# Feed-forwards 2 to 4 of a Conformer trunk: seven of nine inner blocks by seven products, with the weight sums of four of them made in advance

## The chip, the cores and the metric

The kernel runs on one core of a Trainium2 chip. The time is the device time of one execution in microseconds; the time before is the median of three runs, and one further execution was profiled. Everything below is float32: each matrix product is made as three TensorE matmuls of numbers split into a high and a low part.

## The reference

The input is 256 tokens of 1024 features. Two layers follow one another; each is feed-forward, mixer, feed-forward, with residual additions, and a final norm ends it. So there are four feed-forwards, numbered 1 to 4 here. The mixer of the first layer is a convolution module (between feed-forwards 1 and 2), that of the second is latent attention (between 3 and 4).

```
def swiglu_ffn(h, w1, w3, w2):                 # w1, w3: 1024 x 2816, w2: 2816 x 1024
    return (jax.nn.silu(h @ w1) * (h @ w3)) @ w2

for i in range(DEPTH):                          # DEPTH = 2
    h = h + 0.5 * swiglu_ffn(rmsnorm(h, ffn_norm1[i]), ffn1_w1[i], ffn1_w3[i], ffn1_w2[i])
    m = rmsnorm(h, mix_norm[i])
    h = h + (conv_module(m, ...) if i % 2 == 0 else mla(m, ...))
    h = h + 0.5 * swiglu_ffn(rmsnorm(h, ffn_norm2[i]), ffn2_w1[i], ffn2_w3[i], ffn2_w2[i])
return rmsnorm(h, final_norm)
```

## The kernel before, in words

**Weights.** All weights come in blocks of 128 x 2048 floats (1 MB). A list `blocks` names them in the order in which they are used: per feed-forward 22 blocks of w1 and w3 (the gates), then 11 blocks of w2, each of which holds two groups of 128 rows. `load` brings a block from HBM into a `raw` tile through the SP queue; ScalarE casts it to `hi` (L171) and VectorE subtracts to get `lo` (L175). There are four `raw` buffers and four `hi`/`lo` pairs, used in rotation. `weights` hands a block to the products and, by `load_ahead`, issues in program order the loads of the following blocks for which `hi`/`lo` slots are left.

**Splitting a product.** `mm3` makes one product of 128 x 128 by 128 x 512 by three matmuls: high by low, high by high, low by high (L284, L287, L288).

**Gates.** In six steps `c` (five of 512 columns, a last one of 256) the kernel makes u for w1 and w3 and both halves of the tokens (tb = 0, 1), then the gated value g. `turn` transposes g: VectorE turns 32 x 32 squares (L645), four transfers write the result to a DRAM tile `gd` (L649), one reads it back as `gb` (L651). Then it is split into `Gh` and `Gl` (L624, L625), the left operands of the second product. Step `c` yields the operands of the w2 blocks 2c and 2c+1.

**Second product.** `Rows` accumulates in four PSUM banks (two token halves by two column halves). A plain block (`block`) takes eight products, 24 matmuls. The blocks in `FAST`, which are 0, 2, 4, 6 and 8, are made by seven products (`fast`), 21 matmuls, after the scheme of Strassen and Winograd: the 2 x 2 split of tokens and rows by rows and columns. It needs sums of weight quarters and differences of gate quarters, and four extra banks p1, p5, q7, q6. `load_fast` makes the sums of weights in a second `raw` tile, `sums`: one operation on POOL for two of them (L185) and two adds on VectorE (L186, L187), and then splits both tiles (L193, L194), so that such a block takes two `raw` buffers and two `hi`/`lo` slots. `combine` makes the differences of gates on POOL (L632). After the last fast block `fold` adds the extra banks into h, with ScalarE (L572), VectorE (L574 to L579) and POOL (L573 to L580). The last two blocks, 9 and 10, are made bank by bank in `finish`, each followed by an add into h (L587) and by pieces of the next stage's norm.

**Order.** A planner orders the instructions of every engine by a simulated time line; `order` adds an ordering between two instructions of one engine by hand without a wait, and `behind` keeps the work on weights behind the last few urgent pieces. Each engine and the SP queue then run their instructions strictly in that order. All transfers spoken of here are issued by SP.

**End.** In feed-forward 4 the next stage is `Final`: it fetches the final gain `gf` once into its own tile (L484), and each piece of the result is made in one of four tiles `hg`.

Of the kernel before, what the change touches and what calls it, by code (L numbers as in the profile page):

```python
# [45 lines left out]
FAST = (0, 2, 4, 6, 8)  # L46
# [41 lines left out]
def trunk(ctx: ExitStack, tc: tile.TileContext, x, xt, pos, invf, gains, gfin, wdw,  # L88
# [27 lines left out]
    conv_block = {}  # L116
    for i in range(2):
# [35 lines left out]
    def load(src, pieces=1):  # L153
        if isinstance(src, tuple) and src[0] == "fast":
            return load_fast(src[1])
        if isinstance(src, tuple):
# [21 lines left out]
    def load_fast(src):  # L178
# [7 lines left out]
        behind(nc.vector.tensor_add(t[:, 2, :], t[:, 0, :], v[:, 3, :]))  # L186
        behind(nc.vector.tensor_add(t[:, 3, :], t[:, 2, :], v[:, 2, :]))  # L187
# [23 lines left out]
    def slots(b):  # L211
        return 2 if isinstance(blocks[b], tuple) and blocks[b][0] == "fast" else 1
# [267 lines left out]
    class Final:  # L480
        def __init__(self, act):
            self.act = act
            self.gf = act.tile([P, D], F32, tag="gf", name="gf")
            nc.sync.dma_start(self.gf, gfin.partition_broadcast(P))  # L484

            self.e = [None] * NT
            self.n = [0] * NT
            self.y = {}

        def piece(self, tb, c):  # L490

            n = c.stop - c.start
            t = self.act.tile([P, 512], F32, tag="hg", name=uid("hg"), bufs=4)
# [26 lines left out]
    class Rows:  # L520
        def __init__(self, zh, zl, nk, last=False, sh=None, sl=None):
            self.zh, self.zl, self.nk, self.last = zh, zl, nk, last
            self.sh, self.sl = sh, sl
# [24 lines left out]
        def fast(self, i):  # L548

            n = FAST.index(i)  # L550
# [6 lines left out]
            for o, key, (ah, al), (hi, lo), q in (  # L557
                    (self.p[0], "p1", z(f, 0), raw, 0), (self.o[0, 0], (0, 0), z(f + 1, 0), raw, 2),
                    (self.o[0, 1], (0, 1), s(2), raw, 3), (self.p[2], "p5", z(f, 1), sums, 0),
                    (self.p[3], "q7", s(1), sums, 1), (self.p[1], "q6", s(0), sums, 2),  # L560
                    (self.o[1, 0], (1, 0), z(f + 1, 1), sums, 3)):
                c = slice(q * 512, q * 512 + 512)
                mm3(o, ah, al, hi[:, c], lo[:, c], self.begin(key), isinstance(key, str) and i == FAST[-1])
            if i == FAST[-1]:
                self.fold()
# [46 lines left out]
    def ffn(X, make_next, beside=lambda: None):  # L612
        with tc.tile_pool(name=uid("ffn"), bufs=1) as act:
            return ffn_in(act, X, make_next, beside)

    def ffn_in(act, X, make_next, beside):
        Gh = act.tile([P, NF, S], F32R, tag="Gh", name=uid("Gh"))
        Gl = act.tile([P, NF, S], F32R, tag="Gl", name=uid("Gl"))
        Sh = act.tile([P, 3 * len(FAST), P], F32R, tag="Sh", name=uid("Sh"))
        Sl = act.tile([P, 3 * len(FAST), P], F32R, tag="Sl", name=uid("Sl"))  # L620
# [6 lines left out]
        def combine(i, b0, b1):  # L627

            n = FAST.index(i)
            sx = act.tile([P, 4, P], F32, tag="sx", name=uid("sx"))  # L630
            v = sx.rearrange("p s (i q) -> p s i q", q=32)
            sub = lambda o, a, b: nc.gpsimd.tensor_tensor(o, a, b, op=ALU.subtract)  # L632
# [4 lines left out]
            split(Sh[:, 3 * n:3 * n + 3, :], Sl[:, 3 * n:3 * n + 3, :], sx[:, :3, :])  # L637
            split(Gh[:, 2 * i, tbs(1)], Gl[:, 2 * i, tbs(1)], sx[:, 3, :])

        def turn(c, tb, w, g):  # L640
# [10 lines left out]
            nc.sync.dma_start(b[:, :w], d)  # L651
# [3 lines left out]
            t0 = 0  # L655
            if tb == 1 and 2 * c in FAST:
                t0 = 1
                combine(2 * c, first[c], bv)
            f = slice(4 * c + t0, 4 * c + n)
            gh, gl = (G_[:, f, tbs(tb)].rearrange("p t (i q) -> p t i q", q=32) for G_ in (Gh, Gl))  # L660
            split(gh, gl, bv[:, t0:])
# [49 lines left out]
        o = Rows(Gh, Gl, NF, make_next is Final, Sh, Sl)  # L711
        for i in range(NF // 2 - 2):
            (o.fast if i in FAST else o.block)(i)
# [663 lines left out]
```

## Time and profile before

| what | value |
|---|---|
| median of three runs | 924.54 us (923.88 to 925.65) |
| the profiled execution | 923.62 us |
| its span (first to last instruction) | 921.8 us |
| TensorE clock granted | 0.999 of full |
| HBM read, written | 178.17 MB, 12.58 MB |
| feed-forward 2: gates until, second product until | about 404, about 460 us |
| feed-forward 3: gates until, second product until | about 581, about 640 us |
| feed-forward 4: gates until, second product until | about 858, about 915 us |

The page gives for each engine the time in which it was busy; PE is TensorE, PEld its weight loads, DVE is VectorE, ACT ScalarE, POOL GpSimd, SPq the SP queue. In the timelines a row gives the start, the duration, the engine, the line of the kernel, the operation, the tiles written and read, the size, the count, and in brackets how long the engine had been idle and what ended that. Matmuls overlap: one takes 0.39 us from start to end, but the next starts after about 0.23. The second columns of a windows row are busy times in us within the stretch.

### The profile page before, as it was taken

The numbers are of one execution on the slowest core, as the hardware profiler recorded it, in microseconds if no ns is written. First come the engines' busy times: TensorE is split into PE (matmuls) and PEld (weight loads), VectorE is DVE, ScalarE is ACT, GpSimd is POOL, SyncE is SP. The second block draws the span as 40 slices with busy tenths as digits, with TensorE's granted clock in tenths as the row PEclk, the third lists the DMA queues.
The fourth block names the chain that finished last, engine by engine and source line by source line (L and its number), as shares of the span: only waits on it lengthen the run. The fifth ranks groups of instructions, "written<-read, shape, count | busy, mean of one in ns | idle before, by whom it ended". The sixth has DMA issues, their size and how long they took to land.

```text
span 921.8 us, 12383 instructions
## 1 busy us (share of the span) xinstructions
PE 909.6 (99%) x4293; PEld 755.5 (82%) x4293; DVE 680.9 (74%) x1052; ACT 539.7 (59%) x940; POOL 226.4 (25%) x337
## 2 busy tenths in 40 slices
PE   9999999999999999999999999999999999999997
PEld 6888888898958888888888888888998788888886
DVE  5776877689977666777976667978667476667876
ACT  6964556568877455455474544655666475444643
POOL 1101232379941100232300003224200000013223
PEclk9999999999999999999999999999999999999999
DMA  9976656653307676556756775656441557774651
GB/s 342 350 276 226 203 180 222 240 183 138 138 22 283 244 255 240 189 161 228 299 205 238 252 244 153 228 209 214 183 183 60 186 202 251 246 239 150 219 183 47
DMA packets 60399, 191.58 MB, mean 208 GB/s; under 512 B 11184, under 2 KB 33328, under 8 KB 40752
## 3 DMA queue, kind: packets, MB, share of 16 engines
q1 hardware_dynamic: 59760, 190.09, 58.9%
q8 instruction: 34, 0.56, 0.2%
q10 hardware_dynamic: 576, 0.69, 0.2%
q14 instruction: 29, 0.24, 0.1%
HBM read 178.17 MB, written 12.58 MB: 207 GB/s over the span
## 4 chain that ended last, share of the span: by engine, by line
PE 72%; DVE 8%; DMA 8%; ACT 4%; issue 3%; POOL 3%; SPq 1%; POOLq 0%; ACTq 0%; DVEq 0%
PE u L288 15%; PE u L287 15%; PE u L284 15%; DVE lo L175 5%; PE o L284 3%; PE o L287 3%; PE o L288 3%; PE gate L738 3%; DMA raw<-in_f2w 3%; DMA raw<-in_f1w 3%; PE u L738 3%; POOL sums L185 3%; PE o L978 2%; ACT hi L171 1%; DVE lo L194 1%
## 5 line engine op out<-in xcount | busy, mean ns | idle before, releaser
L175 DVE TENSOR_TENSOR lo<-raw,hi 128x1024 fp32r<-128x1024 f32 (+1 forms) x246 | 296.3, 1240 | 74.4 <-ACT hi L171 74.1
L171 ACT CAST hi<-raw 128x1024 fp32r<-128x1024 f32 (+1 forms) x250 | 247.9, 1046 | 147.7 <-PE u L288 107.9
L288 PE MATMUL u<-hi,Xl 128*128 128x512 f32 x688 | 267.8, 390 | 0.7 <-DVE Xl L345 0.7
L284 PE MATMUL u<-lo,Xh 128*128 128x512 f32 x688 | 268.1, 390 | 0.1
L287 PE MATMUL u<-hi,Xh 128*128 128x512 f32 x688 | 267.7, 389 | 0.0
L288 PEld LDWEIGHTS u<-hi,Xl 128*128 128x128 f32 x688 | 129.1, 188 | 28.2 <-DVE Xl L345 1.6
L284 PEld LDWEIGHTS u<-lo,Xh 128*128 128x128 f32 x688 | 129.2, 188 | 27.3 <-DVE lo L175 0.5
L287 PEld LDWEIGHTS u<-hi,Xh 128*128 128x128 f32 x688 | 129.2, 188 | 26.6
L185 POOL TENSOR_TENSOR sums<-raw 128x1024 f32<-128x1024 f32 x20 | 54.2, 2710 | 162.4 <-DMA raw<-in_f2w 52.7
L284 PE MATMUL o<-lo,Gh 128*128 128x512 f32 (+1 forms) x236 | 91.5, 388 | 0.7 <-DVE lo L175 0.7
L287 PE MATMUL o<-hi,Gh 128*128 128x512 f32 (+1 forms) x236 | 91.0, 386 | 0.0
L288 PE MATMUL o<-hi,Gl 128*128 128x512 f32 (+1 forms) x236 | 91.0, 386 | 0.0
L632 POOL TENSOR_TENSOR sx<-gb 128x128 f32<-128x128 f32 x20 | 10.2, 509 | 316.7 <-DMA gb<-gd 316.7
L624 ACT CAST Gh<-gb 128x512 fp32r<-128x512 f32 (+2 forms) x48 | 25.8, 539 | 63.6 <-DMA gb<-gd 63.5
L193 ACT CAST hi<-sums 128x1024 fp32r<-128x1024 f32 x40 | 41.2, 1052 | 30.7 <-PE u L288 14.7
L786 DVE SCALAR_TENSOR_TENSOR acc<-V,dw,acc 128x128 f32<-128x128 f32 (+1 forms) x174 | 57.8, 411 | 0.0
L625 DVE TENSOR_TENSOR Gl<-gb,Gh 128x512 fp32r<-128x512 f32 (+2 forms) x48 | 33.2, 705 | 31.2 <-ACT Gh L624 31.1
L194 DVE TENSOR_TENSOR lo<-sums,hi 128x1024 fp32r<-128x1024 f32 x40 | 56.1, 1432 | 0.0
L284 PEld LDWEIGHTS o<-lo,Gh 128*128 128x128 f32 x236 | 44.3, 188 | 11.0 <-DVE lo L175 2.3
L288 PEld LDWEIGHTS o<-hi,Gl 128*128 128x128 f32 x236 | 44.3, 188 | 8.9
L287 PEld LDWEIGHTS o<-hi,Gh 128*128 128x128 f32 x236 | 44.3, 188 | 8.8
L814 ACT ACTIVATE prod<-V,dw 128x128 f32<-128x128 f32 (+1 forms) x129 | 48.0, 418 | 2.8 <-POOL Y L815 1.4
(247 smaller groups left out, 1325.7 us busy)
## 6 DMA issues: line engine op xcount, KB each, us to landing
raw<-in_f2w SPq DMA_DIRECT2D x66, 1024.0 KB, 4.8
raw<-in_f1w SPq DMA_DIRECT2D x64, 1024.0 KB, 5.0
raw<-in_cw SPq DMA_DIRECT2D x12, 1024.0 KB, 5.2
gd<-gt SPq DMA_DIRECT2D x160, 64.0 KB, 2.7
gb<-gd SPq DMA_DIRECT2D x40, 256.0 KB, 3.4
raw<-in_wo SPq DMA_DIRECT2D x4, 1024.0 KB, 4.8
raw<-in_wuq SPq DMA_DIRECT2D x3, 1024.0 KB, 4.8
raw<-in_f1w SPq DMA_DIRECT2D x8, 256.0 KB, 6.2
```

The costliest lines, as they stand in the source:

```text
L171: behind(nc.scalar.copy(hi[:, c], raw[:, c]))
L175: behind(nc.vector.tensor_sub(lo[:, c], raw[:, c], hi[:, c].bitcast(F32)))
L185: behind(nc.gpsimd.tensor_tensor(t[:, 0:2, :], v[:, 0:4:3, :], v[:, 1:2, :].to_broadcast([P, 2, 512]), op=ALU.add))
L193: behind(nc.scalar.copy(hi[:, c0:c1], x[:, c0:c1]))
L194: behind(nc.vector.tensor_sub(lo[:, c0:c1], x[:, c0:c1], hi[:, c0:c1].bitcast(F32)))
L284: mm = nc.tensor.matmul(o, ah, bl, start=start, stop=False)
L287: nc.tensor.matmul(o, ah, bh, start=False, stop=False)
L288: return nc.tensor.matmul(o, al, bh, start=False, stop=stop)
L625: nc.vector.tensor_sub(dl, x, dh.bitcast(F32))
L738: mm = nc.tensor.matmul(u[:, t], w[:, c], X.x[:, k, t], start=(k == 0), stop=(k == KT - 1))
L786: ins = nc.vector.scalar_tensor_tensor(out if j == j1 - 1 else y, v, w, y, op0=ALU.mult, op1=ALU.add)
L814: prod = nc.scalar.activation(p, v, AF.Copy, scale=w)
```

## The change

Feed-forward 1 stays as it is. In feed-forwards 2 to 4 the fast blocks are now 0, 2, 3, 4, 5, 6 and 7 instead of 0, 2, 4, 6 and 8. For the blocks 3, 4, 6 and 7 the sums of weights are not made when the block is needed, but earlier: behind the loads of the gate blocks 6, 10, 14 and 18 a job (`sum_ahead`) loads the w2 block into a `raw` buffer, makes the four sums in place by four adds on VectorE, and stores the tile to DRAM. Later `load_summed` loads three quarters of the w2 block (the second quarter is not used raw) in two transfers and the stored sums in a third. These loads are ordered on SP behind the load of the last turned gate that has been issued in program order. Blocks 0, 2 and 5 are made as before, in place.

`combine` makes the differences for both blocks of a step in one go where both are fast. The two last sums change places in the tile, and the products that read them with them. The operands `Sh`, `Sl` grow from 15 to 21 slices and `sx` doubles; to make room, the final gain takes the place of `Xl`, and the pieces of the result that of the tiles `gb` and `gt`.

```
-FAST = (0, 2, 4, 6, 8)
+FAST = ((0, 2, 4, 6, 8), (0, 2, 3, 4, 5, 6, 7))
+AHEAD = {3: 6, 4: 10, 6: 14, 7: 18}
...
-            blocks += [("fast", w2[i, a_]) if a_ in FAST else w2[i, a_] for a_ in range(NF // 2)]
+            first = len(blocks) == 22
+            for a_ in range(NF // 2):
+                w = w2[i, a_]
+                if not first and a_ in AHEAD:
+                    jobs[len(blocks) - a_ - 22 + AHEAD[a_]] = (a_, w)
+                    w = ("summed", w, a_)
+                elif a_ in FAST[0 if first else 1]:
+                    w = ("fast", w)
+                blocks.append(w)
...
-        behind(nc.vector.tensor_add(t[:, 2, :], t[:, 0, :], v[:, 3, :]))
-        behind(nc.vector.tensor_add(t[:, 3, :], t[:, 2, :], v[:, 2, :]))
+        behind(nc.vector.tensor_add(t[:, 3, :], t[:, 0, :], v[:, 3, :]))
+        behind(nc.vector.tensor_add(t[:, 2, :], t[:, 3, :], v[:, 2, :]))
+        return split_fast(raw, sums)
+
+    def sum_ahead(a, src):
+        raw = rawp.tile([P, HB], F32, tag="raw", name=uid("job"))
+        nc.sync.dma_start(raw, src)
+        v = raw.rearrange("p (b n) -> p b n", n=512)
+        for to, x, y in ((0, 0, 1), (1, 1, 3), (3, 0, 3), (2, 3, 2)):
+            behind(nc.vector.tensor_add(v[:, to, :], v[:, x, :], v[:, y, :]))
+        summed[a] = dram.tile([P, HB], F32, tag=f"summed{a}", name=uid("summed"))
+        nc.sync.dma_start(summed[a], raw)
+
+    def load_summed(src, a):
+        raw = rawp.tile([P, HB], F32, tag="raw", name=uid("raw"))
+        sums = rawp.tile([P, HB], F32, tag="raw", name=uid("sums"))
+        for c in (slice(0, 512), slice(1024, HB)):
+            order(nc.sync.dma_start(raw[:, c], src[:, c]), last_turned[-1].ins)
+        order(nc.sync.dma_start(sums, summed[a]), last_turned[-1].ins)
+        return split_fast(raw, sums)
...
     def load_to(last):
         while len(loaded) < last:
-            loaded.append(load(blocks[len(loaded)], PIECES))
+            b = len(loaded)
+            loaded.append(load(blocks[b], PIECES))
+            if b in jobs:
+                sum_ahead(*jobs[b])
...
-            self.gf = act.tile([P, D], F32, tag="gf", name="gf")
+            self.gf = xp.tile([P, KT, S], F32, tag="Xl", name="gf").rearrange("p k t -> p (k t)")[:, :D]
...
-            self.early = max(i for i in range(nk // 2 - 2) if sh is None or i not in FAST)
+            self.early = max(i for i in range(nk // 2 - 2) if i not in fasts)
...
-        def combine(i, b0, b1):
+        def combine(c, count, b0, b1):
...
-            sub(v[:, 3], b1[:, 0], b1[:, 1])
-            sub(v[:, 0], b0[:, 0], v[:, 3])
-            sub(v[:, 1], b1[:, 0], b0[:, 0])
-            sub(v[:, 2], b0[:, 1], v[:, 0])
+            even, odd = slice(0, 2 * count, 2), slice(1, 2 * count, 2)
+            sub(v[:, :, 3], b1[:, even], b1[:, odd])
+            sub(v[:, :, 0], b0[:, even], v[:, :, 3])
+            sub(v[:, :, 1], b1[:, even], b0[:, even])
+            sub(v[:, :, 2], b0[:, odd], v[:, :, 0])
...
-            nc.sync.dma_start(b[:, :w], d)
+            last_turned.append(nc.sync.dma_start(b[:, :w], d))
```

`split_fast` is the second half of the old `load_fast`, unchanged.

More of the change, by code (lines that the diff above doesn't have):

```diff
@@ L116, in trunk @@
     conv_block = {}
+    jobs = {}
     for i in range(2):
@@ L155, in load @@
             return load_fast(src[1])
+        if isinstance(src, tuple) and src[0] == "summed":
+            return load_summed(*src[1:])
         if isinstance(src, tuple):
@@ L211, in slots @@
     def slots(b):
-        return 2 if isinstance(blocks[b], tuple) and blocks[b][0] == "fast" else 1
+        return 2 if isinstance(blocks[b], tuple) and blocks[b][0] in ("fast", "summed") else 1
     def load_ahead(ahead=W_BUFS - 2):
@@ L613, in ffn, with ffn_in @@
         with tc.tile_pool(name=uid("ffn"), bufs=1) as act:
[L614 to L616 removed]
+            return ffn_in(act, X, make_next, beside, FAST[0 if X.whole else 1])
+    def ffn_in(act, X, make_next, beside, fasts):
         Gh = act.tile([P, NF, S], F32R, tag="Gh", name=uid("Gh"))
         Gl = act.tile([P, NF, S], F32R, tag="Gl", name=uid("Gl"))
[L619 to L620 removed]
+        Sh = act.tile([P, 3 * len(fasts), P], F32R, tag="Sh", name=uid("Sh"))
+        Sl = act.tile([P, 3 * len(fasts), P], F32R, tag="Sl", name=uid("Sl"))
         first = {}
@@ L654, in turn @@
                 first[c] = bv
[L655 to L661, printed above, removed]
+            own = slice(0, n)
+            if tb == 1 and 2 * c in fasts:
+                count = 2 if 2 * c + 1 in fasts else 1
+                own = slice(1, n, count)
+                combine(c, count, first[c], bv)
+            gh, gl = (G_[:, 4 * c:4 * c + n, tbs(tb)].rearrange("p t (i q) -> p t i q", q=32) for G_ in (Gh, Gl))
+            split(gh[:, own], gl[:, own], bv[:, own])
         for c in range(6):
@@ L710, in ffn_in @@
                 turn(c, tb, w, g)
-        o = Rows(Gh, Gl, NF, make_next is Final, Sh, Sl)
+        o = Rows(Gh, Gl, NF, make_next is Final, Sh, Sl, fasts)
         for i in range(NF // 2 - 2):
-            (o.fast if i in FAST else o.block)(i)
+            (o.fast if i in fasts else o.block)(i)
             beside()
```

31 lines of the change are left out of this document (18 added, 13 removed).

## The prediction

> **What bounds the kernel now.** I read the page first (span, busy shares, chain), then the busy time by stage, then the timelines of TensorE, SP, VectorE and ScalarE around one second product, where the change acts. The page:
>
> ```profile
> span 921.8 us, 12383 instructions
> PE 909.6 (99%) x4293; PEld 755.5 (82%) x4293; DVE 680.9 (74%) x1052; ACT 539.7 (59%) x940; POOL 226.4 (25%) x337
> GB/s 342 350 276 226 203 180 222 240 183 138 138 22 283 244 255 240 189 161 228 299 205 238 252 244 153 228 209 214 183 183 60 186 202 251 246 239 150 219 183 47
> PE 72%; DVE 8%; DMA 8%; ACT 4%; issue 3%; POOL 3%; SPq 1%; POOLq 0%; ACTq 0%; DVEq 0%
> L185 POOL TENSOR_TENSOR sums<-raw 128x1024 f32<-128x1024 f32 x20 | 54.2, 2710 | 162.4 <-DMA raw<-in_f2w 52.7
> raw<-in_f2w SPq DMA_DIRECT2D x66, 1024.0 KB, 4.8
> ```
>
> TensorE is busy 99% of the span: only fewer products, or fewer of its few waits, can shorten it, and any new wait on it is paid in full. The stages of feed-forward 2 (gates, then second product), with two stretches of dense loading (columns: stretch, us, then PE, PEld, DVE, ACT, POOL busy, clock, DMA share, GB/s):
>
> ```profile
> 289.00:404.00 115.00, 115.00 (x509) 95.24 (x508) 80.98 (x89) 58.04 (x73) 15.96 (x18) 1.00 0.66 227
> 404.00:460.00 56.00, 56.00 (x249) 46.37 (x248) 47.92 (x51) 31.64 (x40) 17.72 (x11) 1.00 0.69 242
> 445.00:450.00 5.00, 5.00 (x24) 4.14 (x23) 3.68 (x4) 4.41 (x5) 2.05 (x1) 1.00 1.00 410
> 450.00:455.00 5.00, 5.00 (x24) 4.14 (x23) 5.00 (x6) 2.08 (x3) 1.77 (x2) 1.00 0.96 388
> ```
>
> In the second product VectorE works 48 of 56 us, so it is the engine closest behind. The DMA engines move 227 to 242 GB/s there, and 410 when loads queue back to back.
>
> **Part 1, the products.** A block by seven products has 21 matmuls instead of 24. The cadence comes from the first matmul of block 0 and the first of block 3 (21+24+21 = 66 matmuls later):
>
> ```profile
> 404.13 0.39 PE L284 MATMUL p<-lo,Gh 128*128 128x512 f32 x1
> ...
> 419.09 0.39 PE L284 MATMUL o<-lo,Gh 128*128 128x512 f32 x1
> ```
>
> 14.96 / 66 = 0.2267 us. Each feed-forward 2 to 4 goes from five such blocks to seven: 3 x 2 x 3 = 18 matmuls fewer, -4.08 us. A fast block lasts 4.76 us, a plain one 5.44.
>
> **Part 2, three waits that should go.**
>
> ```profile
> 462.79 0.50 PE L288 MATMUL u<-hi,Xl 128*128 128x512 f32 x1 [0.28 <-DVE Xl L345]
> 641.29 0.50 PE L288 MATMUL a<-hi,Xl 128*128 128x512 f32 x1 [0.28 <-DVE Xl L345]
> 894.28 0.50 PE L284 MATMUL o<-lo,Gh 128*128 128x512 f32 x1 [0.23 <-DVE lo L175]
> ...
> 453.68 4.17 DVE L175 TENSOR_TENSOR lo<-raw,hi 128x1024 fp32r<-128x1024 f32 x2
> 457.78 0.68 DVE L579 TENSOR_TENSOR fold<-p,fold 128x512 f32<-128x512 f32 x1
> 458.38 1.87 DVE L587 TENSOR_TENSOR h<-o,h 128x512 f32<-128x512 f32 x3
> ```
>
> The adds into h stand three in a row at 458.38, late, behind the fold and two splits. The fold follows the last fast block; that becomes block 7 instead of 8, so it starts 6.8 us earlier (after six fast and one plain block, 34.0 us, instead of four and four, 40.8). Each wait costs its idle time plus 0.11 (the matmul after it takes 0.50 instead of 0.39): 0.39 + 0.39 + 0.34 = 1.1 us. I count all of it, -1.1 (between 0 and -1.1); late next is nothing until the last product itself.
>
> **Part 3, the sums beside the gates.** Twelve jobs (four per feed-forward). Each adds on SP a load and a store of 1 MB, and on VectorE four 128x512 adds. For those the nearest row is the present add:
>
> ```profile
> L186 DVE TENSOR_TENSOR sums<-sums,raw x20: 674/692/694, 102.9 to 890.7; 128x512 f32<-128x512 f32 x20
> 315.32 11.25 SPq L168 DMA_DIRECT2D raw<-in_f2w  x3
> 333.61 2.00 ACT L171 CAST hi<-raw 128x1024 fp32r<-128x1024 f32 x2 [3.44 <-PE u L288]
> 334.69 2.36 DVE L175 TENSOR_TENSOR lo<-raw,hi 128x1024 fp32r<-128x1024 f32 x2 [2.79 <-ACT hi L171]
> ```
>
> 4 x 4 x 0.69 = 11.0 us of VectorE per gate stage, on top of 80.98 of 115: 0.80 busy. DMA: 4 x 2.1 MB = 8.4 MB in 115 us, 73 GB/s more, 300 in all, under 410. What covers it: the load issued at 315.32 lands 4.8 us later and its cast starts only at 333.61 (four raw buffers, four casts 5.44 apart), when a product frees its slot; the split is then used three blocks later. So a load has some 13 us to spare and a split some 12. A job takes one of the four raw buffers (5.4 us of that slack) for its load, adds and store, about 4.8 + 3 + 4.8 = 12.6 us; a store that waits on SP for the adds holds the next load and the gate turns behind it by about 3 us. All of it fits: 0. If the cover failed, by 1 us a job, +12. I take 0.
>
> **Part 4, small edits.** The rows:
>
> ```profile
> L632 POOL TENSOR_TENSOR sx<-gb x20: 457/463/825, 44.4 to 859.4; 128x128 f32<-128x128 f32 x20
> 453.23 1.29 POOL L576 TENSOR_TENSOR h<-h,fold 128x512 f32<-128x512 f32 x1 [3.50 <-DVE fold L575]
> L484 SPq DMA_DIRECT2D gf<-in_gfin x1: 328/328/328, 735.1 to 735.1; - x1
> L498 DVE TENSOR_TENSOR hg<-h,gf x5: 424/684/693, 909.0 to 916.3; 128x512 f32<-128x512 f32 x3, 128x256 f32<-128x256 f32 x2
> ...
> 410.19 4.56 DVE L194 TENSOR_TENSOR lo<-sums,hi 128x1024 fp32r<-128x1024 f32 x2
> 409.88 2.66 POOL L185 TENSOR_TENSOR sums<-raw 128x1024 f32<-128x1024 f32 x1 [2.15 <-DVE lo L194]
> 420.56 2.34 DVE L194 TENSOR_TENSOR lo<-sums,hi 128x1024 fp32r<-128x1024 f32 x2
> ```
>
> The same two subtractions take 4.56 us beside POOL's sum and 2.34 without it. [...]
>
> POOL's differences for a pair of blocks are 128x256, between the 0.46 of 128x128 and the 1.29 of 128x512, about 0.74: three pairs and one single block take 12 x 0.74 + 4 x 0.46 = 10.7 us where five singles took 20 x 0.46 = 9.2, in a stage where POOL is busy for 16 of 115: 0. Of the in-place sums, those of blocks 4, 6 and 8 go and that of block 5 comes, net two fewer per feed-forward: 2 x 2.7 us less on POOL and 4 x 0.69 less on VectorE. The two extra fast blocks split a sums tile each (2.34) and leave out a quarter of the raw one (0.6). VectorE per second product: 47.92 - 2.8 + 2 x 1.75 = 48.7 of 54.6 us, tighter but still under: 0. The final gain, fetched at 735.1 until now, must wait until the gates of feed-forward 4 have read Xl; its first use is at 909.0, a whole second product later: 0. The swapped order of the two last sums and the later add of the one bank that only plain blocks fill: 0.
>
> **Part 5, the reload, where the price is.** Blocks 3, 4, 6 and 7 now load 0.75 MB of raw weights and 1 MB of sums, and these may be issued only behind the load of the last turned gate. Until now block 3's load went out at 399.33:
>
> ```profile
> 399.33 0.39 SPq L168 DMA_DIRECT2D raw<-in_f2w  x1
> ...
> 412.41 0.34 SPq L651 DMA_DIRECT2D gb<-gd  x1
> 414.78 0.35 SPq L168 DMA_DIRECT2D raw<-in_f2w  x1
> ...
> 414.56 0.41 ACT L624 CAST Gh<-gb 128x256 fp32r<-128x256 f32 x1 [1.85 <-DMA gb<-gd]
> 416.62 1.05 ACT L193 CAST hi<-sums 128x1024 fp32r<-128x1024 f32 x1 [0.18 <-PE o L288]
> ```
>
> Now it cannot go before 412.41 + 0.4, 6.3 us ahead of block 3's first matmul at 419.09, where it had 20. That last gate, 0.13 million bytes, lands 2.15 us after issue (412.41 to 414.56), of which 1.8 pass before its bytes move. In the queue stand 0.13 + 0.79 + 1.05 = 2.0 million bytes, 4.8 us at 410 GB/s: the sums land at 412.4 + 1.8 + 4.8 = 419.0. Cast 1.05, subtraction 1.2 (half of 2.34) and 0.1 between them make the first half ready at 421.4. Block 3 needs it after its three raw products, 9 x 0.2267 later: 421.13. So 0.3 us are missing; ScalarE and VectorE take the raw halves and the last gates first, so I take 0.8. The bounds: 0, if the gates turn 0.5 us sooner; or transfers that pass one at a time at the median's 4.8 us for 1 MB: raw at 416.6 (three quarters of 4.8 after 413.0), sums at 421.4, ready at 423.7, 2.6 missing. I stand near the low end because three loads are queued together, which is the 410 row.
>
> Block 4 follows 1.835 million bytes later, 4.5 us: sums at 423.6, ready at 425.9, needed at 419.09 + 0.8 + 4.76 + 2.04 = 426.7: just in time. Block 5 makes its sums in place; its buffer comes free with block 3's raw split, about 419.4; behind block 4 it lands at 426.2, then POOL 2.4, two adds 1.3, cast 1.05, subtraction 1.2: 432.2, needed at 432.8. Blocks 6 and 7 wait for buffers likewise. New stall: 3 x 0.8 = +2.4 (0 to 7.8).
>
> **The sum.** -4.08 - 1.1 + 2.4 = -2.8 us on the profiled execution of 923.62 us (span 921.8 and 1.8 around it). That execution lies 0.9 below the median 924.54; on the median the forecast is 921.7.
>
> **Rivals.**
> 1. The reload is hidden. For it: the gates' last turn has less beside it on VectorE and POOL (no sums for block 4 at 409.88). Then -5.2: 919.3.
> 2. The reload runs slower than TensorE eats: 1.835 million bytes per 4.76 us are 385 GB/s, just under the rows of 388 and 410. At 342, the first slice of the page, block 3 comes 1.0 later and block 4 another 0.6 (5.37 against 4.76); block 5's small load gives it back. 2.4 per feed-forward: +7.2 - 5.2 = +2.0, 926.5. Against it: both dense rows.
> [...]
> 3. Slower: the load behind the last turned gate becomes the wait of every second product. Place: block 3, then block 5's chain with 0.6 us of margin. It decides from 1.7 us per feed-forward on (5.2 / 3), and is slower by over 0.2% from 2.4. With the upper bound 2.6 and another 1 at blocks 4 to 7: 3 x 3.6 - 5.2 = +5.6, 930.1. For it: 14 us of lead are given up, and VectorE is 0.9 busy there.
> 4. The jobs hold up the gates through SP's order or a raw buffer: 1 us each, +12 - 2.8, 933.7. Against it: the 12 to 13 us of slack.
>
> **How the numbers follow.** A measurement of this kernel tells about 0.2%, 1.85 us, from no change: below 922.7 is faster, above 926.4 slower. Forecast with stalls of 0.3 to 1.1: 0.38. Hidden: 0.17. Rate: 0.15, two thirds of it within 0.2%, the rest slower. Late reload: 0.23, of which 0.06 lies between 1.1 and 2.4 and so within 0.2%. Jobs: 0.07, slower. Faster 0.55, same 0.16, slower 0.29. The range: low end all stalls gone less the run spread (923.88 against 924.54), 918.7; high end the late reload and the spread upward (925.65), 931. The likeliest case alone spans 920.2 to 922.6.
>
> **What would show it.** Right: o and p matmuls 18 fewer; fold 6 to 7 us earlier; no wait on Xl at the two transitions; a wait of the block-3 matmul on a subtraction of sums, under 1 us, three times; the gates at 115 us as before. Wrong: waits over 2.4 us in blocks 3 to 7, ended by the load of sums or by the subtractions behind it; or gate stages longer than 115.

## The result, and the profile after

The changed kernel takes 963.12 us (median of six runs, 960.48 to 967.89) against 924.76 beside it (922.08 to 925.65). The ratio over all runs is 1.0428, with a 95% interval of 1.0391 to 1.0465. So it is 38.4 us slower, where 2.8 faster was forecast. The profiled execution after took 960.48 us (span 958.7), 36.9 above that of before.

The page of the changed kernel, its busy times (share of the span, instructions):

```profile
span 958.7 us, 12493 instructions
PE 917.8 (96%) x4275; PEld 752.7 (79%) x4275; DVE 728.4 (76%) x1094; ACT 549.8 (57%) x946; POOL 226.6 (24%) x319
```

TensorE has its 18 matmuls fewer (4275 against 4293). It is idle instead. The waits of TensorE (us in total, times, the longest):

```profile
PE o L326 <- DVE g L753: 12.2, 3, 6.6
PE p L326 <- DVE lo L233: 11.3, 10, 2.0
PE o L326 <- DVE lo L233: 2.8, 5, 1.2
...
PE o L326 <- DVE lo L189: 1.1, 3, 0.4
```

These four, 27.4 us, stand in the second products; the kernel before had hardly any there. From the first to the last matmul in the timelines, the second products of feed-forwards 2, 3 and 4 took 56.4, 56.4 and 57.3 us and now take 65.4 (402.7 to 468.1), 69.1 (590.5 to 659.6) and 72.4 (878.8 to 951.2): 36.8 us more, the whole loss. The gate stages are as long as they were (120.6 to 121.0 us from the first gate matmul to the first of the second product).

Two kinds of waits stand out. The first is new: the last product of block 0 needs the PSUM bank in which the last gate step was accumulated, and that bank comes free only when VectorE has made g from it. The same stretch on three engines of the changed kernel, feed-forward 3 (start, duration, engine, and in brackets the idle time before and what ended it):

```profile
593.49 0.62 ACT L667 CAST Gh<-gb 128x512 fp32r<-128x512 f32 x1 [7.45 <-DMA gb<-gd]
...
596.57 0.62 ACT L667 CAST Gh<-gb 128x512 fp32r<-128x512 f32 x1 [0.56 <-DMA gb<-gd]
597.10 0.83 ACT L751 ACTIVATE s<-u,R 128x256 f32<-128x256 f32 x2
...
597.97 0.48 DVE L753 SCALAR_TENSOR_TENSOR g<-u,rh,s 128x256 f32<-128x256 f32 x1
...
598.51 0.79 PE L326 MATMUL o<-lo,Gh 128*128 128x512 f32 x1 [3.78 <-DVE g L753]
```

On ScalarE the silu of the last step (597.10) stands behind the casts of the step before, and these wait for turned gates, 7.45 us for the first. TensorE finds the bank taken. So gates that are turned late cost TensorE nothing in the gate stage, and 3.78 us just behind it.

The second kind is the wait of blocks 3 to 7 on their splits (`lo`, L233). The loads of blocks 3 and 4 in feed-forward 2 of the changed kernel, SP above, ScalarE's casts below:

```profile
414.86 0.34 SPq L696 DMA_DIRECT2D gb<-gd  x1
...
416.19 0.43 SPq L223 DMA_DIRECT2D sums<-summed  x1
416.73 0.90 SPq L222 DMA_DIRECT2D raw<-in_f2w  x2
...
422.64 1.99 ACT L232 CAST hi<-sums 128x1024 fp32r<-128x1024 f32 x2 [1.68 <-DMA sums<-summed]
```

The last turned gate goes out at 414.86 (412.41 before), and ScalarE waits for the sums until 422.64, where 419.0 was forecast. The second product itself begins 1.4 us sooner than before (402.73 against 404.13). Counted from its first matmul the last turned gate goes out after 12.1 us instead of 8.3, and ScalarE has the sums after 19.9 where 14.9 was forecast. Block 3 and its followers wait in turn.

A wait also costs more than its row says. Three matmuls of the changed kernel:

```profile
420.76 0.40 PE L330 MATMUL p<-hi,Gl 128*128 128x512 f32 x1
422.27 0.50 PE L326 MATMUL o<-lo,Gh 128*128 128x512 f32 x1 [1.11 <-DVE lo L233]
422.61 0.39 PE L329 MATMUL o<-hi,Gh 128*128 128x512 f32 x1
```

From 420.76 to 422.61 pass 1.85 us for two steps of 0.227, so the wait costs 1.40, not 1.11: idle time is counted from the end of the last matmul, 0.16 after the next could have begun, and the restart takes 0.11 more. The prediction had only the 0.11. For 21 waits this is some 6 us.

### The profile page after: what moved, and what is told of

It is laid out like the page before. It is cut to its first block, busy times and chain, and to the rows that moved or that the text cites. A ratio compares the mean times of both kernels' runs of the same rounds, so it can differ in the third digit from the quotient of the medians.

```text
span 958.7 us, 12493 instructions
## 1 busy us (share of the span) xinstructions
PE 917.8 (96%) x4275; PEld 752.7 (79%) x4275; DVE 728.4 (76%) x1094; ACT 549.8 (57%) x946; POOL 226.6 (24%) x319
## 4 chain that ended last, share of the span: by engine, by line
PE 41%; DMA 24%; DVE 19%; ACT 7%; issue 4%; SPq 3%; POOL 1%; DVEq 0%; POOLq 0%; ACTq 0%
DMA gb<-gd 8%; DVE lo L189 7%; PE u L330 6%; PE u L326 5%; DMA sums<-summed 5%; PE u L329 5%; DMA gd<-gt 4%; PE o L326 4%; PE o L329 3%; PE o L330 3%; DVE lo L233 3%; DVE job L214 2%; ACT hi L185 2%; DMA raw<-in_f2w 2%; DMA raw<-in_f1w 2%
## 5 line engine op out<-in xcount | busy, mean ns | idle before, releaser
L189 DVE TENSOR_TENSOR lo<-raw,hi 128x1024 fp32r<-128x1024 f32 (+1 forms) x234 | 286.8, 1264 | 45.1 <-ACT hi L185 44.6
L185 ACT CAST hi<-raw 128x1024 fp32r<-128x1024 f32 (+1 forms) x238 | 235.5, 1045 | 105.3 <-PE u L330 82.7
L326 PE MATMUL o<-lo,Gh 128*128 128x512 f32 (+1 forms) x200 | 80.2, 403 | 16.1 <-DVE g L753 12.2
L675 POOL TENSOR_TENSOR sx<-gb 128x256 f32<-128x256 f32 (+1 forms) x17 | 15.4, 907 | 307.8 <-DMA gb<-gd 307.8
L199 POOL TENSOR_TENSOR sums<-raw 128x1024 f32<-128x1024 f32 x14 | 37.5, 2678 | 179.2 <-DMA raw<-in_f2w 91.0
L329 PE MATMUL o<-hi,Gh 128*128 128x512 f32 (+1 forms) x200 | 78.7, 393 | 0.0
L330 PE MATMUL o<-hi,Gl 128*128 128x512 f32 (+1 forms) x200 | 78.0, 391 | 0.0
L233 DVE TENSOR_TENSOR lo<-sums,hi 128x1024 fp32r<-128x1024 f32 x52 | 63.6, 1257 | 15.9 <-ACT hi L232 15.9
L232 ACT CAST hi<-sums 128x1024 fp32r<-128x1024 f32 x52 | 52.2, 1048 | 34.2 <-DMA sums<-summed 18.8
L233 DVE TENSOR_TENSOR lo<-raw,hi 128x512 fp32r<-128x512 f32 (+1 forms) x52 | 57.2, 1126 | 10.8 <-ACT hi L232 10.8
L232 ACT CAST hi<-raw 128x512 fp32r<-128x512 f32 (+1 forms) x52 | 41.6, 834 | 20.5 <-DMA raw<-in_f2w 7.5
L214 DVE TENSOR_TENSOR job<-job 128x512 f32<-128x512 f32 x48 | 37.6, 783 | 20.4 <-DMA job<-in_f2w 15.0
```

The costliest lines, as they stand in the source:

```text
L185: behind(nc.scalar.copy(hi[:, c], raw[:, c]))
L189: behind(nc.vector.tensor_sub(lo[:, c], raw[:, c], hi[:, c].bitcast(F32)))
L199: behind(nc.gpsimd.tensor_tensor(t[:, 0:2, :], v[:, 0:4:3, :], v[:, 1:2, :].to_broadcast([P, 2, 512]), op=ALU.add))
L214: behind(nc.vector.tensor_add(v[:, to, :], v[:, x, :], v[:, y, :]))
L232: behind(nc.scalar.copy(hi[:, c0:c1], x[:, c0:c1]))
L233: behind(nc.vector.tensor_sub(lo[:, c0:c1], x[:, c0:c1], hi[:, c0:c1].bitcast(F32)))
```

## The experiments

Three theories to start with; the expectations call them A, B and C. **Jobs** (A): making the sums beside the gates delays the gates' turning. **Order** (B): the loads held behind the last turned gate come too late. **Row** (C): seven fast blocks, six of them in a row, are too much for the engines that prepare their operands, whatever the loads do. The kernel before ran beside every group at 923.3 to 924.0 us.

### The reload without the jobs, and the jobs without the reload

The first run drops the jobs and lets the third load bring the block instead of its sums:

```
-                    jobs[len(blocks) - a_ - 22 + AHEAD[a_]] = (a_, w)
...
-        order(nc.sync.dma_start(sums, summed[a]), last_turned[-1].ins)
+        order(nc.sync.dma_start(sums, src), last_turned[-1].ins)
```

> Leaves the jobs out: no load, adds and store beside the gates; the third load of blocks 3, 4, 6 and 7 brings the block itself in place of the stored sums, so that the same bytes come at the same place (the sums are not made, the result is not the reference's). Theory A (the jobs beside the gates make the last gates late, the wait for banks at the start of the second product and the late reload both follow from it): no wait of TensorE on the gating operation (12.2 us before), waits in blocks 3 to 7 at most 1.5 us per feed-forward, 919 to 927 us. Theory B (the reload behind the last turned gate is late by itself): the bank wait goes, but the waits in blocks 3 to 7 stay at 4 to 6 us per feed-forward, 933 to 945 us. Theory C (seven blocks by seven products overload VectorE and ScalarE): nothing gained against the changed kernel but the bank wait, over 940 us.

The second keeps the five fast blocks of before, their sums in place, and runs the jobs beside them for nothing:

```
-FAST = ((0, 2, 4, 6, 8), (0, 2, 3, 4, 5, 6, 7))
+FAST = ((0, 2, 4, 6, 8), (0, 2, 4, 6, 8))
...
-                    w = ("summed", w, a_)
-                elif a_ in FAST[0 if first else 1]:
+                if a_ in FAST[0 if first else 1]:
```

> Five fast blocks made in place as in the kernel before, and the twelve jobs (load, four adds, store) beside the gates, whose stored sums nobody reads. Theory A: the wait of TensorE on the gating operation at the start of the second products comes here too, 2 to 7 us each with a lower granted clock behind it, 938 to 950 us. Theory B: no such wait, 923 to 928 us. Theory C: as B.

Measured: 946.41 without the jobs (1.0245, 1.0226 to 1.0264; +22.9 us) and 938.66 with the jobs alone (1.0172, 1.0147 to 1.0198; +15.1). Together 38.0, and the change costs 38.4: the two halves of the change add up, so they are separate causes. The first half still holds both the order and the row; at 946.41 it lies just above the range of theory B and in that of C. The waits of TensorE with the reload alone:

```profile
PE p L325 <- DVE lo L232: 7.4, 9, 1.7
PE o L325 <- DVE lo L232: 5.5, 6, 2.6
```

and with the jobs alone:

```profile
PE o L325 <- DVE g L752: 5.1, 2, 2.8
```

In these two runs the wait on g belongs to the jobs, and that on the splits of blocks 3 to 7 to the reload.

### Seven blocks in place, and the loads set free

Is the reload worse than what it replaces? All seven sums made in place, no jobs:

```
-                if not first and a_ in AHEAD:
+                if False:
```

> Seven fast blocks, the sums of all made in place on POOL and VectorE when the block is loaded; no jobs, no reload. Theory A and B: no bank wait at the start; VectorE has 5.2 us of work per fast block against TensorE's 4.76, so that blocks 4 to 7 fall behind by some 0.5 us each and POOL's 2.4 us lies in the chain of each: 922 to 932 us. Theory C: over 940 us.

And the changed kernel without the order behind the last turned gate:

```
-            order(nc.sync.dma_start(raw[:, c], src[:, c]), last_turned[-1].ins)
-        order(nc.sync.dma_start(sums, summed[a]), last_turned[-1].ins)
+            nc.sync.dma_start(raw[:, c], src[:, c])
+        nc.sync.dma_start(sums, summed[a])
```

> The changed kernel without the ordering of the reload behind the last turned gate: the planner may issue it as soon as buffers are free. Theory A: the bank waits at the start stay (some 12 us in all) and cost most of the time, 945 to 965 us. Theory B: the waits in blocks 3 to 7 fall from about 5 to under 2 us per feed-forward, 940 to 950 us.

Measured: 949.41 in place (1.0277, 1.026 to 1.0294) and 946.47 with the loads free (1.0247, 1.0231 to 1.0262). In place is thus no better than the reload alone (946.41), and in the range of theory C. The order alone costs 963.1 - 946.5 = 16.6 us, or 15.4 when each is compared with the kernel before beside it. The waits of TensorE with the loads free:

```profile
PE o L326 <- DVE g L753: 11.4, 3, 7.0
PE p L326 <- DVE lo L233: 3.1, 5, 1.4
```

Those on the splits shrink from 14.1 (11.3 + 2.8) to 3.1; those on g stay. In place, VectorE has more to do than TensorE. Its operations of that run in the second product of feed-forward 2, by shape (busy us, mean ns):

```profile
L233 DVE TENSOR_TENSOR lo<-sums,hi 128x1024 fp32r<-128x1024 f32 x12 | 15.4, 1303 | 0.0
L201 DVE TENSOR_TENSOR sums<-sums,raw 128x512 f32<-128x512 f32 x5 | 7.8, 1551 | 0.0
L233 DVE TENSOR_TENSOR lo<-raw,hi 128x1024 fp32r<-128x1024 f32 x6 | 7.3, 1211 | 0.0
L233 DVE TENSOR_TENSOR lo<-raw,hi 128x512 fp32r<-128x512 f32 x6 | 4.1, 679 | 0.0
L200 DVE TENSOR_TENSOR sums<-sums,raw 128x512 f32<-128x512 f32 x5 | 3.4, 681 | 2.3 <-POOL sums L199 2.3
```

A fast block takes 2 x 1.303 + 1.211 + 0.679 + 0.681 + 1.551 = 6.73 us of VectorE, while TensorE eats one in 21 x 0.2267 = 4.76. Over the five that follow block 2 without a plain one between, that is 9.8 us a feed-forward (an estimate). The kernel before never met this: each fast block there had a plain one behind it.

### What in the jobs costs

Jobs alone again, without the additions, and without the store:

```
-        for to, x, y in ((0, 0, 1), (1, 1, 3), (3, 0, 3), (2, 3, 2)):
-            behind(nc.vector.tensor_add(v[:, to, :], v[:, x, :], v[:, y, :]))
```

> The kernel with the jobs only, whose jobs load a block and store it again without the four adds (nobody reads the store). If the transfers of the jobs make the gates late (theory A1), the waits on the gating operation stay and the time is near that of the jobs with adds: 933 to 941 us. If VectorE's adds do it (theory A2): no such wait, 923 to 928 us.

```
-        summed[a] = dram.tile([P, HB], F32, tag=f"summed{a}", name=uid("summed"))
-        nc.sync.dma_start(summed[a], raw)
```

> The kernel with the jobs only, whose jobs load a block and make the four adds but store nothing. If the store and its wait on the SP queue are what holds the gates (theory A1s): back to 923 to 928 us. If the load in front of the turned gates does it (theory A1l): 930 to 940 us. If the adds (theory A2): 933 to 941 us.

Measured: 926.75 without the additions (1.004, 1.0023 to 1.0057) and 936.46 without the store (1.0141, 1.012 to 1.0163). So the traffic without additions costs 3 us in all, and the additions, where they stand, the other 12.

Then the order on the engines: the casts of the last-but-one gate step behind the silu and the gating of the last, in the changed kernel, and the same with the loads free:

```
+                if both:
+                    for high, low in held:
+                        order(high, silu.ins)
+                        order(low, gate.ins)
```

> The changed kernel with two orderings by hand in feed-forwards 2 to 4: ScalarE's casts of the fifth step's turned gates come behind the two activations of the last step, and VectorE's subtractions behind its gating. Theory A (the activation stands behind casts that wait for a late transfer): the wait for banks (12.2 us in three places) goes, the last gates turn 2 to 7 us sooner and the reload with them; what stays is about the cost of the reload alone, 940 to 950 us. If the gates are late for another reason, the wait stays and the time is 955 to 965 us.

> Both: the two orderings of the run with gates first, and the reload not held behind the last turned gate. Theory A with B: 946.5 us less the bank waits (11.4 us) and the slow clock behind them (some 6 us), 925 to 933 us. If one of the two only moves the wait elsewhere: 938 to 950 us.

Measured: 956.35 (1.0353, 1.0324 to 1.0381) and 946.49 (1.0232, 1.0198 to 1.0266), the latter as much as with the loads free alone. The waits of TensorE in the former:

```profile
PE p L326 <- DVE lo L233: 12.0, 10, 2.3
PE o L326 <- DVE lo L233: 6.5, 6, 2.1
PE o L326 <- DVE g L757: 1.7, 1, 1.7
```

The wait on g is nearly gone (12.2 to 1.7), but the splits wait longer (14.1 to 18.5). So the bank of the last gate is where the lateness shows, not where it comes from: the turned gates are late, and whatever stands first, something waits.

Why do additions of 3 us a job make them late? Two candidates: VectorE, which runs its instructions in the program's order, stands idle before the additions until the job's load lands (20.4 us in the changed kernel); or it is the work itself. First the additions given to GpSimd, then those on VectorE held behind the transposes of the gate step before, both with the jobs alone:

```
-            behind(nc.vector.tensor_add(v[:, to, :], v[:, x, :], v[:, y, :]))
+            behind(nc.gpsimd.tensor_tensor(v[:, to, :], v[:, x, :], v[:, y, :], op=ALU.add))
```

> Jobs alone on the five products of before, as in the run with jobs only (938.66 us), but the four additions of a job made by GpSimd instead of VectorE. If the jobs cost what they do because of VectorE (its time, or its standing in order in front of a job's load), the time falls to that of the run without additions, 926.75, or up to 930. [...]

```
+            add = nc.vector.tensor_add(v[:, to, :], v[:, x, :], v[:, y, :])
+            behind(add)
+            order(add, last_squares[-1].ins)
```

> Jobs alone again, the additions on VectorE as in the change, but each ordered behind the transposes of the gate step before it, so that VectorE comes to them with the load landed and with its gating done. If VectorE's wait in order for the job's load is what delays the gating (idle of 20.4 us before these additions in the changed kernel), the time is 927 to 931. If VectorE's 37.6 us of additions themselves are what it has no room for, it stays at 936 to 939.

Measured: 973.81 on GpSimd (1.0544, 1.0508 to 1.058) and 940.94 held (1.0194, 1.015 to 1.0237). Neither run is faster than the jobs as first written, and the second lies above both ranges expected of it. The additions with the jobs alone, as first written (the last figures are VectorE's idle time before them):

```profile
L213 DVE TENSOR_TENSOR job<-job 128x512 f32<-128x512 f32 x48 | 35.2, 733 | 8.5 <-DMA job<-in_f2w 7.6 <-DMA job<-in_f1w 0.5
```

and held:

```profile
L214 DVE TENSOR_TENSOR job<-job 128x512 f32<-128x512 f32 x48 | 32.6, 680 | 0.8
```

VectorE's idle time has gone and the time has not, so the wait in order is not the cause by itself. It does not fall altogether, because this run also holds each job's buffer longer (below). On GpSimd:

```profile
L213 POOL TENSOR_TENSOR job<-job 128x512 f32<-128x512 f32 x48 | 79.0, 1646 | 192.6 <-DMA job<-in_f2w 125.5 <-issue 33.7 <-DMA job<-in_f1w 18.8
```

VectorE is rid of 35 us of additions there, and the kernel is slower by 35 us more. This does not clear VectorE's own work: its busy time fell by only 12 us (710.9 to 698.9), because its other operations took longer beside GpSimd's, as two subtractions of the kernel before did (4.56 us beside GpSimd's sum, 2.34 without it). The 128x384 subtraction of the turned gates, for one, took 1.44 us on average instead of 0.75 in feed-forward 2. TensorE waited inside the gate stages too (9.2 us for s, 8.2 for g). So this run changes more than the place of the additions, and it decides nothing about VectorE.

Both runs make a job last longer; on GpSimd its additions take 6.6 us instead of 2.9. What a job holds meanwhile is one of four buffers for fresh weights, and SP. The waits of the SP queue for jobs, jobs alone:

```profile
SPq L215 <- DVE job L213: 51.3, 12, 6.7
```

on GpSimd:

```profile
SPq L215 <- POOL job L213: 90.4, 11, 9.4
```

and held, where it is the next load of weights that waits for the job's buffer:

```profile
SPq L181 <- DMA summed<-job: 88.8, 12, 9.2
```

In these waits, up to 6.7, 9.4 and 9.2 us long, SP issues neither weights nor gates, and towards the end of the gates the weights may be behind. Windows of 370 to 390 us, in feed-forward 2 (busy us and counts of PE, PEld, DVE, ACT, POOL; clock; DMA share; GB/s); the kernel before:

```profile
370.00:390.00 20.00, 20.00 (x90) 16.57 (x89) 14.68 (x18) 10.50 (x14) 6.15 (x5) 1.00 0.55 176
```

jobs without additions:

```profile
370.00:390.00 20.00, 20.00 (x90) 16.57 (x89) 17.11 (x18) 10.59 (x14) 6.71 (x5) 1.00 0.63 210
```

jobs alone:

```profile
370.00:390.00 20.00, 20.00 (x90) 16.53 (x89) 14.02 (x18) 8.45 (x11) 4.23 (x4) 1.00 0.86 311
```

Read this way, two have caught up by then; the third still loads at 311 GB/s, and the work on those weights meets the last two gate steps. If that is the cause, a job that is issued one gate step earlier should cost next to nothing:

```
-AHEAD = {3: 6, 4: 10, 6: 14, 7: 18}
+AHEAD = {3: 2, 4: 6, 6: 10, 7: 14}
```

> Jobs alone on the five products of before, each one gate step (four blocks of weights) earlier: behind blocks 2, 6, 10, 14 instead of 6, 10, 14, 18. If a job costs because it holds one of the four buffers for fresh weights from its load to the end of its store, so that the weights fall behind and are still being caught up in the last gate step (370 to 390 us moves 311 GB/s in the run with jobs only, against 176 in the kernel before), the last step is free again and the time is 925 to 931. If VectorE has no room for 12 us of additions in each feed-forward wherever they stand, it stays at 936 to 941.

Measured: 925.75 (1.0028, 1.0015 to 1.0041), +2.4 us instead of +15.1, with the same additions on the same engine. TensorE has no wait on g left. SP's waits for jobs in this run:

```profile
SPq L181 <- DMA summed<-job: 21.9, 11, 4.6
SPq L215 <- DVE job L213: 2.0, 5, 1.3
```

So the jobs' cost depends on where they stand, and VectorE has room for the additions when they come early. Why the place matters is not settled, as no single quantity above explains it:

- The jobs are not shorter: from a job's load to its store pass 15 to 38 us here, and 8 to 15 with the jobs alone.
- VectorE's idle time before the additions has gone (8.5 to 0.6 us), but so it did in the held run, which stayed slow.
- SP's waits for jobs fell to 25.2 us in all, from 58.1 with the jobs alone. But without the additions they came to 60.9 (29.6 before the next load of weights, 31.3 before the jobs' own stores), at a cost of 3.0 us. Two of their rows in that run:

```profile
SPq L181 <- DMA summed<-job: 29.6, 7, 6.2
SPq L213 <- DMA job<-in_f2w: 18.6, 7, 5.0
```

- The rate at 370 to 390 us does not order the runs: without the store it is 231 GB/s at a cost of 12.7 us, with the early jobs 263 at 2.4.

What goes with the cost, roughly, is how late the last turned gate is. From the first matmul of the second product of feed-forward 2 to the issue of its load pass 8.3 us in the kernel before, 8.6 with early jobs, 9.2 without additions, 12.0 without the store, 15.4 held, 16.6 with the jobs alone and 17.0 on GpSimd. The early jobs also leave more time behind them: the last store of feed-forward 2 goes out 47 us ahead of the second product, against 29 with the jobs alone.

### What is left: the row of fast blocks

No jobs and no order (the third load brings the block itself, as in the first run):

```
-                    jobs[len(blocks) - a_ - 22 + AHEAD[a_]] = (a_, w)
...
+            nc.sync.dma_start(raw[:, c], src[:, c])
+        nc.sync.dma_start(sums, src)
```

> No jobs, and the three loads of blocks 3, 4, 6, 7 issued as early as their buffers allow instead of behind the last turned gate (a third load of the right size brings the block itself instead of its sums, so the result is not the reference's). If the order behind the last turned gate is what the reload costs (946.41 with it), the time is 922 to 930, the seven products with it at no loss or a gain. If six fast blocks in a row have no slack for their casts, differences and loads, whatever the order, it stays at 936 or more.

Then the changed kernel with the loads free, with the additions held, and with the jobs earlier:

> The changed kernel with both undone that cost: loads issued without the order behind the last turned gate (946.47 so), and the additions of the jobs held behind the transposes of the gate step before. If the wait in order on VectorE is the cause of the late gating, 928 to 936. If VectorE has no room for the additions at all, 943 to 947.

> The changed kernel with loads issued without the order behind the last turned gate (946.47 alone) and with each job one gate step earlier. If the late catching up of the weights is what is left of the jobs' cost, the time is that of the run without jobs, 929.27, and 1 to 6 more: 930 to 935. If the additions cost VectorE wherever they stand, 942 to 947.

Measured: 929.27 with neither jobs nor order (1.0058, 1.0041 to 1.0075), 953.05 free and held (1.0316, 1.0279 to 1.0353), 933.11 free and earlier (1.0103, 1.0084 to 1.0122). The order costs 946.41 - 929.27 = 17.1 us without the jobs, about as much as with them (16.6). Free loads and earlier jobs take back 28.6 of the 38.4: what is left is 9.8 above the kernel beside it. Holding the additions made it worse than free loads alone (946.47), against both ranges expected; SP waits 89.9 us for the buffers of held jobs there, but that this is the reason is not shown. Even with both causes out the seven products lose: 5.5 us more than before with 18 matmuls fewer. Windows of the kernel without jobs and order, second product of feed-forward 2:

```profile
420.00:428.00 8.00, 8.00 (x37) 6.52 (x36) 8.00 (x8) 5.26 (x6) 2.51 (x1) 1.00 0.58 197
428.00:436.00 8.00, 7.92 (x34) 5.90 (x33) 7.96 (x9) 5.69 (x7) 0.00 (x0) 1.00 0.88 312
436.00:444.00 8.00, 7.14 (x32) 5.59 (x31) 5.35 (x6) 4.30 (x5) 0.00 (x0) 1.00 0.91 359
444.00:452.00 8.00, 8.00 (x37) 6.44 (x36) 7.58 (x9) 6.49 (x7) 2.95 (x2) 1.00 0.98 386
```

VectorE is busy without a break for 16 us (8.00, 7.96), then the transfers run at 359 to 386 GB/s, near the 385 at which TensorE eats such blocks. The kernel before has windows as full without any wait (VectorE 8.00 of 8 us at 436 to 444, 399 GB/s at 444 to 452), but there they do not follow each other. That a row of six leaves room in neither is argued from these windows, and no run separates VectorE from the transfers. So would a row of three do? Blocks 0, 2, 4, 6, 7, 8, once all in place, once with the sums of block 7 made by one early job and loaded freely:

```
-FAST = ((0, 2, 4, 6, 8), (0, 2, 3, 4, 5, 6, 7))
+FAST = ((0, 2, 4, 6, 8), (0, 2, 4, 6, 7, 8))
...
-AHEAD = {3: 6, 4: 10, 6: 14, 7: 18}
+AHEAD = {7: 6}
```

> Six products' blocks instead of seven in feed-forwards 2 to 4: 0, 2, 4, 6, 7, 8, so three fast blocks in a row instead of six; all sums made in place, no jobs and no third load. Nine matmuls fewer than before: -2.0 us (9 x 0.2267). If only a row of six is too long for casts, differences and loads (949.41 with seven blocks in place), 921 to 926. If any fast block without a plain one behind it costs its share, a third of the 25.9 us that seven in place cost, 930 to 934.

> The same six blocks, with the sums of block 7 alone made ahead, by one job behind block 6 of the gates, and loaded without the order behind the last turned gate. If the jobs and the reload are cheap where they are early and few (925.75 for four early jobs alone), and three fast blocks in a row are carried with the sums ready, 920 to 924. If the casts and differences of three fast blocks in a row are too much with the sums ready as well, 927 or more.

Measured: 935.2 in place (1.0124, 1.0107 to 1.0141) and 931.09 with one job (1.0078, 1.0063 to 1.0093). The waits of TensorE in the latter:

```profile
PE tp L369 <- DVE h L630: 3.2, 2, 1.6
PE p L326 <- DVE lo L233: 2.1, 3, 1.5
```

Here the largest wait is on the adds into h (L630) at the end of the second product, which stand behind VectorE's splits. The blocks themselves pass in the time of before: from the first to the end of the last matmul the second products take 56.5, 56.6 and 57.9 us, against 56.6, 56.6 and 57.3. But after the first two of them the next stage starts 60.4 and 60.6 us behind that first matmul, where it was 57.7. So the loss lies in the change of stage. This agrees with VectorE being short of time where fast blocks follow each other, but it does not prove it; block 8 was fast before too. None of the versions tried beats the kernel before.

## Why the prediction was wrong

- **Part 1** (18 matmuls fewer, -4.08): the count is right. The gain is nowhere in the time: TensorE waits instead.
- **Part 2** (three waits gone, -1.1): wrong. The two waits on Xl are still there, 0.42 us each (at 470.64 and 662.21) where they were 0.28, and the third has become three of 0.36 to 0.37 (the row of L189 above). The fold was to come 6.8 us earlier. Its first add into h on POOL now starts 45.7 us behind the first matmul of the second product (448.45), where before it was 43.6 (447.69), because the stalls ahead of it used that up.
- **Part 3** (jobs at no cost, "+12 if the cover failed"): failed. The jobs alone cost 15.1; that this is near the 12 is luck, as it came in a few waits of TensorE behind the gates and not as 1 us a job. The step that failed is "All of it fits: 0". The slack of 12 to 13 us was read at 315 to 333 us, early in the gate stage, and applied to all four jobs as if each found it whole. A job's load and additions were put at 4.8 + 3 us; in the changed kernel 8 to 17 us pass from its load to its store. The last turned gate came 3.8, 6.6 and 9.2 us later in the three second products than before, counted from their first matmuls. One gate step earlier the jobs cost 2.4 us; by which way the place acts stays open. The price in VectorE's time, 11 us per feed-forward on an engine 0.80 busy, was right and is not what costs, as the early jobs show. The rival for this had a chance of 0.07, and the place it named, SP's order or a raw buffer, is where long waits were found.
- **Part 5** (reload, 0.8 a feed-forward, bounds 0 to 2.6): wrong by a factor of about seven: the order costs 16.6 to 17.1 us, some 5.6 a feed-forward. Three steps failed. The loads of block 4 were taken to pass behind those of block 3, but some of their bytes moved in between: the windows of the run with the reload alone, from 409.9 to 419.1 us, add up to 2.7 million bytes, where 1.97 stood up to and with block 3's sums (an estimate). In the run with the reload alone, the last turned gate, the sums of block 3 (411.21), the loads of block 4 and the cast that waits for block 3's sums:

```profile
409.88 0.34 SPq L695 DMA_DIRECT2D gb<-gd  x1
...
411.21 0.43 SPq L222 DMA_DIRECT2D sums<-in_f2w  x1
411.76 0.92 SPq L221 DMA_DIRECT2D raw<-in_f2w  x2
...
419.06 1.99 ACT L231 CAST hi<-sums 128x1024 fp32r<-128x1024 f32 x2 [1.55 <-DMA sums<-in_f2w]
```

  From the last turned gate's issue (409.88) to this cast pass 9.2 us, where 6.6 were worked out; the upper bound (9.0) took single transfers at the median. The last turned gate was taken at its time before, though in the changed kernel the jobs put it later, as under part 3. And blocks 4 to 7 were put at no wait at all: in the run with the reload alone block 3 took 6.9, 8.9 and 9.7 us instead of 4.76, 11.2 too many in all, and blocks 4 to 8 a further 7 more than in the run without the order.
- **VectorE's room** (part 4, "48.7 of 54.6, tighter but still under: 0"): the average over the second product hid a row of six blocks, each with 6.7 us of VectorE in place, or 4.7 with the sums loaded (the splits of the run without jobs and order), for every 4.76 of TensorE. This is the likeliest step behind the 5.5 us that stay with jobs and order out and the gain that does not come; it is argued from the windows, and not isolated.
- **Rivals.** The third (late reload) was the right mechanism at 930.1, the fourth at 933.7; they came together, and each was larger. The second, a transfer rate below what TensorE eats, is at most a part: with the same bytes and no order the time is 929.27, and the window from 444 to 452 us above moves 386 GB/s, as much as the 385 that TensorE eats.

## What to carry to other kernels

Treat slack as a stock, not a rate: work slipped beside a stage draws it down, and here the same work cost 15.1 us or 2.4 by its place alone. So place such work with time to catch up behind it, and price the last piece before a change of stage by itself. When a pattern changes from alternating to a row, compare demand and supply inside the row (here VectorE against TensorE per block), not over the stage. An order that is put in to keep urgent transfers ahead can cost the whole lead of what stands behind it; look first at what that lead was hiding.

## What the runs showed of the hardware

The granted TensorE clock fell after some of these waits. A window of the changed kernel behind its longest, 6.56 us (the clock is the third figure from the end):

```profile
890.00:894.00 4.00, 3.60 (x9) 2.86 (x10) 3.97 (x7) 3.29 (x4) 0.00 (x0) 0.50 0.25 41
```

Until 895.26 matmuls follow each other at 0.43 us instead of 0.23: 11 of them in 4.86 us, 2.4 us lost beyond the wait. The wait of 3.78 us in feed-forward 3 cost 1.6 us so (eight matmuls in 3.46 us), and the mean clock of the whole execution fell from 0.999 to 0.992. Behind the wait of 3.78 us, too, the granted clock is 0.50 (598.5 to 600.0 us). The same half pace follows shorter waits, as one of 2.23 us in the run with held additions:

```profile
410.31 0.80 PE L328 MATMUL o<-lo,Gh 128*128 128x512 f32 x1 [2.23 <-DVE g L755]
410.90 0.63 PE L331 MATMUL o<-hi,Gh 128*128 128x512 f32 x1
```

And the pace may fall only after the work has begun again, as in the run with the additions on GpSimd, where the matmuls after a wait of 3.55 us keep theirs for 1.3 us and then slow down:

```profile
401.98 0.51 PE L325 MATMUL u<-lo,Xh 128*128 128x512 f32 x1 [3.55 <-ACT s L750]
...
403.26 0.53 PE L329 MATMUL u<-hi,Xl 128*128 128x512 f32 x1
403.59 0.63 PE L325 MATMUL u<-lo,Xh 128*128 128x512 f32 x1
```

In the timelines of TensorE of the changed kernel and of eleven experiments (five of them in part), from feed-forward 2 on, all 19 waits of 2.23 us or more were followed by a stretch at half the pace (0.43 us from matmul to matmul), which began at the restart or up to 1.6 us behind it and ended 2.7 to 6.1 us after the restart. Of the 14 waits from 1.80 to 2.20 us seven were; the shorter ones were not, unless another wait stood at most 2.6 us ahead.
